# Recurrent mixer of a bidirectional encoder: the work of a block is timed from its own x projection, with four gate buffers, fixed padded convolution inputs and the convolution ranked first

## The chip, the cores and the metric

The kernel runs on one core of one Trainium2 chip. The metric is the device time of one execution in microseconds (us). Three runs of the kernel before took 2115.84, 2116.88 and 2120.38 us; their median is 2116.88 us.

## The reference

An encoder trunk of two residual layers on 256 tokens of width 2048, all in float32. Layer 0 mixes tokens by grouped-query attention, layer 1 by a recurrent block; a SwiGLU network of width 5632 follows each. The change concerns the recurrent mixer alone:

```python
xy = h @ w_in                                   # 2048 -> 2 x 2048
xb, yb = jnp.split(xy, 2, axis=-1)
yb = jax.nn.gelu(yb, approximate=True)
xb = depthwise_conv_centred(xb, conv_w, conv_b) # width 4, over time
h_fwd = rg_lru(xb, w_a[0], b_a[0], w_i[0], b_i[0], lam[0], reverse=False)
h_bwd = rg_lru(xb, w_a[1], b_a[1], w_i[1], b_i[1], lam[1], reverse=True)
out = (h_fwd + h_bwd).astype(h.dtype) * yb
return out @ w_out

# rg_lru: r, i = sigmoid(block_diag(x, w_a) + b_a), sigmoid(block_diag(x, w_i) + b_i)
# a = exp(-8 r softplus(-lam)); u = sqrt(1 - a^2) * (i * x); h_t = a_t h_{t-1} + u_t
```

The gate projections are block diagonal: 8 blocks of 256 channels, each with its own four 256 x 256 matrices (two directions, r and i).

## The kernel before, in words

Activations lie with features on the 128 partitions and the 256 tokens along the free axis. A float32 product is made of three float32r products: each operand is split into hi (rounded) and lo (the rest), and hi x hi, hi x lo and lo x hi are summed in PSUM. Weights arrive by DMA in halves of 8 tiles (`raw`, 512 KB, L92); ACT casts a half to `hi` (L93), VectorE subtracts to get `lo` (L94); each has 5 buffers.

**PE** is the only engine whose order is written out by hand; all others are ordered at build time by a scheduler that estimates times, and by priority, which follows the order of the code. What an engine then gets is a fixed queue: it executes in that order, and an instruction that waits holds up everything behind it.

A **step** is one of the 16 pieces of contraction of a projection. In the mixer `project_sum` issues three matmuls of 128x256 per step (L166 to L168). After each step a clock counts up, and at most one piece of work that is due is issued there; `later(t, fn)` makes `fn` due t steps on.

The mixer works in **blocks** of 256 channels (two tiles of 128). An iteration b (L633) first projects the x branch of block b+1 (`conv_branch`, two projections, 32 steps), then the gate branch of block b (`gelu_branch`, two projections, 32 steps). Between these steps stands the work of block b, by the list `WHEN`: four gates (`gates`, 12 matmuls each, L166 to L168 on `pm<-xs`), four `decay`, four `scan`, then `gelu` and two `finish`. In detail:

- `conv_branch` (L530): VectorE scales the projection into the middle of a padded tile `cb` (L535), whose borders POOL sets to zero (L533, L534). ACT makes the first of four taps `xc` (L537), VectorE adds the other three (L539) and splits the sum into `xs` (L203, L204), which the gates' matmuls read.
- `gates` (L583): matmuls on `xs`, then on ACT a Sigmoid per tile into `sg` (and a Tanh into `th` for the r gates); for the i gates POOL multiplies by `xc` (L599).
- `load_gates` (L556): a DMA into `graw` (256 KB, 2 buffers), ACT's cast `ghi` (L564), POOL's `glo` (L565). With 3 buffers the weights of gate n+3 are loaded once gate n's matmuls have been issued.
- `decay` (L606): Exp on ACT, a square (L610), VectorE's product `th` (L611).
- `scan` (L613): Sqrt on ACT, VectorE's `th` times gate (L616), the scan itself (L619 forward, L621 backward), POOL's sum of the two directions (L622).
- `gelu` (L575) and `finish` (L625): Sigmoid of the gate branch, products on POOL (for the last block on VectorE), split into `act` tiles for the output projection, which starts with 44 steps that need no tile of the last block.

Sigmoid and Tanh, Exp, and Sqrt belong to different activation tables, and `table_op` chains all table users in the order of the code, so that on ACT a block's four Exp come after the Sigmoid of its last gate.

Of the kernel before, what the change touches and what calls it, by code (L numbers as in the profile page):

```python
# [15 lines left out]
ALU = mybir.AluOpType  # L16
AX = mybir.AxisListType

P = 128
S = 256  # L20
# [19 lines left out]
VALUE = 32  # L40
USUAL = (17, 22, 15, 7)
LATE = ((10, 23, 15, 13), (4, 15, 17, 9))
GATE_BUFS = 3
WHEN = (18, 25, 32, 39, 42, 46, 50, 54, 58, 60, 62, 64, 66, 70, 74)
WHEN_LAST = (5, 9, 13, 17, 19, 20, 21, 24, 24, 25, 26, 27, 33, 39, 39)
GELU_B = 0.044715

PK = {}
# [11 lines left out]
def trunk(ctx, tc, w, out):  # L60
    nc = tc.nc
    act, dve, pool, pe, sync = nc.scalar, nc.vector, nc.gpsimd, nc.tensor, nc.sync
# [11 lines left out]
    def nm(s):  # L74
        uid[0] += 1
        return f"{s}_{uid[0]}"

    def tmp(tag, shape=(P, S), dt=F32, bufs=2):
        pl = tp if tag in COMMON else scope[-1]
        return pl.tile(list(shape), dt, tag=tag, name=nm(tag), bufs=bufs)  # L80
# [56 lines left out]
    def later(delay, fn):  # L137
        waiting.append((clock[0] + delay, fn))
# [26 lines left out]
    def three(o, hi, lo, x, start, stop):  # L165
        pe.matmul(o, hi, x[:, :S], start=start, stop=False)  # L166
        pe.matmul(o, hi, x[:, S:], start=False, stop=False)  # L167
        pe.matmul(o, lo, x[:, :S], start=False, stop=stop)  # L168

    def project_sum(xs):  # L170
        acc = new_acc()[:, :S]
        for k0 in range(0, len(xs), HALF):
            for k, (hi, lo) in enumerate(half(), k0):
                three(acc, hi, lo, xs[k], k == 0, k == len(xs) - 1)
                step()
        return acc
# [25 lines left out]
    def split(dst, src):  # L202
        dve.tensor_copy(dst[:, :S], src)  # L203
        dve.tensor_tensor(dst[:, S:], src, dst[:, :S].bitcast(F32), ALU.subtract)  # L204
# [17 lines left out]
    def col(name, i):  # L222
        o = PK[name] + i
        return pk[:, o : o + 1]
# [63 lines left out]
    def table_op(i):  # L288
        if prev[0] is not None:
            tc.add_manual_dep(  # L290
                i.ins, prev[0].ins.name,
                mybir.DependencyInfo(mybir.DependencyClass.NoSync, mybir.DependencyReason.DATA),
                reason="activation tables",
            )
        prev[0] = i

    def table_act(*a, **k):
        table_op(act.activation(*a, **k))  # L298
# [228 lines left out]

    rt = ctx.enter_context(ExitStack())
    scope.append(rt.enter_context(tc.tile_pool(name="rp", bufs=2)))
    def conv_branch(ct):  # L530
        acc = project_sum(nr.xs)
        b = tmp("cb", (P, S + 4))
        pool.memset(b[:, 0:2], 0.0)  # L533
        pool.memset(b[:, S + 2 : S + 4], 0.0)  # L534
        dve.tensor_tensor(b[:, 2 : S + 2], acc, nr.r, ALU.mult)  # L535
        xc = tmp("xc", bufs=4)
        act.activation(xc, b[:, 0:S], AF.Identity, bias=col("conv_b", ct), scale=col("conv_w", ct))  # L537
        for k in range(1, 4):
            dve.scalar_tensor_tensor(xc, b[:, k : k + S], col("conv_w", KT * k + ct), xc, ALU.mult, ALU.add)  # L539
        xs = tmp("xs", (P, 2 * S), F32R, bufs=4)  # L540
        split(xs, xc)
        return xc, xs

    def gelu_branch(ct):
        acc = project_sum(nr.xs)
        y = tmp("fg")
        dve.tensor_tensor(y, acc, nr.r, ALU.mult)
        t = tmp("fu")
        act.activation(t, y, AF.Square)
        dve.scalar_tensor_tensor(t, t, 1.0 / GELU_B, y, ALU.add, ALU.mult)  # L550
        return y, t
# [4 lines left out]
    def load_gates(n):  # L556
        if n >= 4 * NBLK:
            return
        b, g = divmod(n, 4)
        lo = tmp("glo", (P, 4, P), F32R, bufs=GATE_BUFS)  # L560
        hi = tmp("ghi", (P, 4, P), F32R, bufs=GATE_BUFS)
        raw = tmp("graw", (P, 4, P), bufs=2)
        sync.dma_start(out=raw, in_=w["w_gates"][b, :, 4 * g : 4 * g + 4, :])
        act.copy(hi, raw)  # L564
        pool.tensor_tensor(lo, raw, hi[:].bitcast(F32), ALU.subtract)  # L565
        gate_w[n] = hi, lo

    class Block:
# [6 lines left out]
        def gelu(self):  # L575
            table_op(act.preload_act_table_set("sigmoid_and_others"))
            for y, t in self.ys:
                table_act(t, t, AF.Sigmoid, scale=2.0 * GELU_C * GELU_B)
                gl = tmp("gl")
                self.eng.tensor_tensor(gl, y, t, ALU.mult)  # L580
                self.gls.append(gl)

        def gates(self, g):  # L583
            b = self.b
# [2 lines left out]
            for j in range(2):  # L587
                o = pst[:, j * S : (j + 1) * S]
                for k in range(2):
                    m = 2 * k + j  # L590
                    x = self.xcs[k][1]
                    three(o, hi[:, m, :], lo[:, m, :], x, k == 0, k == 1)
            load_gates(4 * b + g + GATE_BUFS)
            for j in range(2):
# [18 lines left out]
        def scan(self, d, j):  # L613
            a, th = self.gate[d, j], self.th[d, j]
            table_act(th, th, AF.Sqrt)
            dve.tensor_tensor(th, th, self.gate[2 + d, j], ALU.mult)  # L616
            h = tmp("h", bufs=4)
            if d == 0:
                dve.tensor_tensor_scan(h, a, th, 0.0, ALU.mult, ALU.add)  # L619
            else:  # L620
                dve.tensor_tensor_scan(h[:, ::-1], a[:, ::-1], th[:, ::-1], 0.0, ALU.mult, ALU.add)  # L621
                self.eng.tensor_tensor(self.hs[j], self.hs[j], h, ALU.add)  # L622
            self.hs.setdefault(j, h)
# [7 lines left out]
    units = [(d, j) for j in range(2) for d in range(2)]  # L631
    blk = nxt = None
    for b in range(-1, NBLK):  # L633
        blk, nxt = nxt, Block(b + 1) if b + 1 < NBLK else None
        if blk:
            work = [partial(blk.gates, g) for g in range(4)]
            work += [partial(blk.decay, *u) for u in units]
            work += [partial(blk.scan, *u) for u in units]
            work += [blk.gelu] + [partial(blk.finish, j) for j in range(2)]
            when = WHEN if nxt else WHEN_LAST  # L640
            for t, fn in zip(when, work):
                later(t, fn)
        if nxt:
            nxt.xcs = [conv_branch(2 * b + 2 + i) for i in range(2)]
            if not blk:
                for g in range(GATE_BUFS):
                    load_gates(g)
        if blk:
            blk.ys = [gelu_branch(2 * b + i) for i in range(2)]

    def end_recurrence():
        rt.close()
        scope.pop()
# [71 lines left out]
```

## Time and profile before

| | |
|---|---|
| median of three runs | 2116.88 us |
| the profiled execution | 2129.33 us, of which 2127.6 us are the span of the profile |
| PE busy | 2085.5 us (98%) |
| VectorE (DVE) busy | 1502.9 us (71%) |
| ACT busy | 1050.4 us (49%) |
| POOL busy | 473.4 us (22%) |
| mixer, from the first gate matmul to the first matmul of the output projection | 1063.31 to 1293.72 us |

The profiled execution is 12.4 us longer than the median; durations are taken from it, and differences are carried over to the median. A row of a timeline has start, duration, engine, line and operation, output <- inputs, and in brackets the idle time before it with what ended it. A duration overlaps the next start a little, so the time that an operation costs in a full queue is read from start to start. A row of waits has the total, the count and the longest.

### The profile page before, as it was taken

How to read it: one execution, taken by the hardware profiler on the slowest of the kernel's cores; microseconds unless marked ns; L12 is line 12 of the kernel's file. 1: busy time of each engine (PE TensorE's matmuls, PEld its weight loads, DVE VectorE, ACT ScalarE, POOL GpSimd, SP SyncE). 2: the span in 40 equal slices, each digit the busy share in tenths (PEclk: the TensorE clock that was granted, in tenths of full speed). 3: DMA queues.
4: the chain of work that ended last, by engine and by line, in shares of the span. 5: the costliest groups of instructions: out<-in, count | busy, mean ns of one | idle time of the engine just before them, and what ended most of it. 6: DMA issues, size and time to landing. Idle time of an engine off the chain costs nothing.

```text
span 2127.6 us, 32676 instructions
## 1 busy us (share of the span) xinstructions
PE 2085.5 (98%) x12512; PEld 1848.4 (87%) x12512; DVE 1502.9 (71%) x2192; ACT 1050.4 (49%) x1598; POOL 473.4 (22%) x454
## 2 busy tenths in 40 slices
PE   7899999999999999999999998999999999999999
PEld 6788888888888888888999997888888888888888
DVE  8899876666566666668889898866666566666665
ACT  5465544443344434444587877454443444444442
POOL 5564431110011100113345553411110011001100
PEclk9999999999999999999999999999999999999999
DMA  6433655555555555555645454555555555665564
GB/s 239 146 122 118 203 187 189 185 185 186 187 188 188 173 186 195 188 183 177 196 160 169 161 166 157 185 188 190 190 194 189 189 189 187 183 203 190 188 189 138
DMA packets 112045, 384.27 MB, mean 181 GB/s; under 512 B 12560, under 2 KB 14736, under 8 KB 111888
## 3 DMA queue, kind: packets, MB, share of 16 engines
q1 hardware_dynamic: 111744, 382.17, 54.4%
q8 instruction: 98, 1.61, 0.3%
q14 instruction: 59, 0.48, 0.1%
q10 hardware_dynamic: 144, 0.02, 0.0%
HBM read 380.04 MB, written 2.10 MB: 180 GB/s over the span
## 4 chain that ended last, share of the span: by engine, by line
PE 86%; DVE 6%; issue 3%; ACT 2%; DMA 1%; POOL 1%; SPq 0%; ACTq 0%; DVEq 0%; POOLq 0%
PE acc L155 53%; PE acc L156 27%; DVE lo L94 2%; DMA graw<-in_w_gates_dram 1%; PE acc L168 1%; PE acc L167 1%; ACT sg L298 1%; PE acc L166 1%; PE pm L167 1%; POOL hb L351 1%; DVE xc L539 1%; PE pm L168 1%; DVE h L621 1%; ACT hi L93 1%; PE pm L166 1%
## 5 line engine op out<-in xcount | busy, mean ns | idle before, releaser
L94 DVE TENSOR_TENSOR lo<-raw,hi 128x1024 fp32r<-128x1024 f32 (+2 forms) x721 | 901.0, 1250 | 509.0 <-ACT hi L93 495.8
L93 ACT CAST hi<-raw 128x1024 fp32r<-128x1024 f32 (+2 forms) x721 | 740.8, 1029 | 928.2 <-PE acc L155 533.6
L155 PE MATMUL acc<-xg,hi 128*128 128x512 f32 x3200 | 1133.1, 398 | 5.7 <-ACT hi L93 5.7
L156 PE MATMUL acc<-xg,lo 128*128 128x256 f32 x3200 | 900.7, 281 | 5.4 <-DVE lo L94 5.4
L155 PEld LDWEIGHTS acc<-xg,hi 128*128 128x128 f32 x3200 | 603.4, 189 | 144.3 <-ACT hi L93 5.7
L155 PE MATMUL acc<-act,hi 128*128 128x512 f32 x1892 | 664.9, 396 | 4.6 <-DVE act L204 4.6
L156 PEld LDWEIGHTS acc<-xg,lo 128*128 128x128 f32 x3200 | 607.8, 190 | 7.1 <-DVE lo L94 7.0
L156 PE MATMUL acc<-act,lo 128*128 128x256 f32 x1892 | 530.9, 281 | 0.4 <-DVE lo L94 0.4
L155 PEld LDWEIGHTS acc<-act,hi 128*128 128x128 f32 x1892 | 355.8, 188 | 87.8 <-DVE act L204 5.5
L497 POOL TENSOR_TENSOR fg<-fg,nr 128x256 f32<-128x256 f32 x88 | 126.1, 1433 | 1189.9 <-ACT fg L298 1189.9
L156 PEld LDWEIGHTS acc<-act,lo 128*128 128x128 f32 x1892 | 358.4, 189 | 0.7 <-DVE lo L94 0.7
L168 PE MATMUL acc<-xg,lo 128*128 128x256 f32 x512 | 146.0, 285 | 3.0 <-DVE lo L94 3.0
L166 PE MATMUL acc<-xg,hi 128*128 128x256 f32 x512 | 146.4, 286 | 2.2 <-ACT hi L93 2.2
L167 PE MATMUL acc<-xg,hi 128*128 128x256 f32 x512 | 145.9, 285 | 0.0
L168 PEld LDWEIGHTS acc<-xg,lo 128*128 128x128 f32 x512 | 99.2, 194 | 3.8 <-DVE lo L94 3.8
L166 PEld LDWEIGHTS acc<-xg,hi 128*128 128x128 f32 x512 | 99.2, 194 | 3.1 <-ACT hi L93 3.1
L167 PEld LDWEIGHTS acc<-xg,hi 128*128 128x128 f32 x512 | 99.1, 194 | 0.0
L280 DVE TENSOR_TENSOR x<-x,acc 128x256 f32<-128x256 f32 x126 | 52.9, 420 | 57.8 <-PE acc L156 57.8
L254 POOL TENSOR_TENSOR ss<-ss,sq 128x256 f32<-128x256 f32 x60 | 78.1, 1302 | 4.9 <-ACT sq L250 0.7
L252 POOL TENSOR_TENSOR sq<-x 128x256 f32<-128x256 f32 x45 | 34.6, 769 | 114.6 <-DVE x L281 112.6
L244 DVE SCALAR_TENSOR_TENSOR xg<-x,pk,xg 128x256 fp32r<-128x256 f32 x64 | 56.2, 891 | 5.2 <-POOL xg L243 5.2
L351 POOL TENSOR_TENSOR hb<-hy,rope 32x256 f32<-32x256 f32 x60 | 46.1, 769 | 44.7 <-DVE hv L419 37.9
(164 smaller groups left out, 1486.6 us busy)
## 6 DMA issues: line engine op xcount, KB each, us to landing
raw<-in_w_gate_dram SPq DMA_DIRECT2D x176, 512.0 KB, 3.6
raw<-in_w_up_dram SPq DMA_DIRECT2D x176, 512.0 KB, 3.6
raw<-in_w_down_dram SPq DMA_DIRECT2D x128, 512.0 KB, 3.6
raw<-in_w_in_dram SPq DMA_DIRECT2D x64, 512.0 KB, 4.0
raw<-in_w_down_dram SPq DMA_DIRECT2D x64, 384.0 KB, 3.1
raw<-in_w_qv_dram SPq DMA_DIRECT2D x40, 512.0 KB, 3.7
raw<-in_w_o_dram SPq DMA_DIRECT2D x32, 512.0 KB, 3.6
raw<-in_w_out_dram SPq DMA_DIRECT2D x32, 512.0 KB, 3.7
```

Source lines behind the costliest of these rows:

```text
L93: act.copy(hi[:, sl, :], raw[:, sl, :])
L94: dve.tensor_tensor(lo[:, sl, :], raw[:, sl, :], hi[:, sl, :].bitcast(F32), ALU.subtract)
L155: pe.matmul(acc, hi, xs[k], start=(k == 0), stop=False)
L156: pe.matmul(acc[:, S:], lo, xs[k][:, :S], start=False, stop=(k == total - 1))
L166: pe.matmul(o, hi, x[:, :S], start=start, stop=False)
L167: pe.matmul(o, hi, x[:, S:], start=False, stop=False)
L168: pe.matmul(o, lo, x[:, :S], start=False, stop=stop)
L244: dve.scalar_tensor_tensor(t[:, S:], x_sb[k], g, t[:, :S].bitcast(F32), ALU.mult, ALU.subtract)
L254: pool.tensor_tensor(self.ss, self.ss, sq, ALU.add)
L280: dve.tensor_tensor(x_sb[j], x_sb[j], acc[:, :S], ALU.add)
L351: eng.tensor_tensor(b[32 * j : 32 * j + 32], y[32 * i : 32 * i + 32], s[32 * i : 32 * i + 32], ALU.mult)
L497: pool.tensor_tensor(g, g, norm.r, ALU.mult)
```

## The change

- `GATE_BUFS` goes from 3 to 4: the weights of gate n+4 are loaded once gate n's matmuls are issued, a whole block ahead.
- The work of a block is no longer started at the head of the iteration after its x branch, but right after its own x branch. The times in `WHEN` count from there: gates at 20, 27, 34, 41 (for the first block 12 less), `decay` and `scan` behind them. `gelu` and `finish` have a list of their own, `WHEN_OUT`, that counts from the end of the gate branch.
- The padded tiles are two fixed ones, cleared once; POOL's 32 small memsets go.
- The convolution behind its projection gets a priority raised by 200.
- Two products are written in place (the GELU product into `y`, the backward scan into its gate tile), so the buffers of `gl` and half of `h` go.

```diff
-GATE_BUFS = 3
-WHEN = (18, 25, 32, 39, 42, 46, 50, 54, 58, 60, 62, 64, 66, 70, 74)
-WHEN_LAST = (5, 9, 13, 17, 19, 20, 21, 24, 24, 25, 26, 27, 33, 39, 39)
+GATE_BUFS = 4
+WHEN = (20, 27, 34, 41, 44, 47, 50, 53, 57, 59, 61, 63)
+FIRST_BLOCK = 12
+AHEAD = 200
+WHEN_OUT = (2, 6, 10)
...
+    padded = [tmp(f"cb{i}", (P, S + 4), bufs=1) for i in range(2)]
+    for b in padded:
+        pool.memset(b, 0.0)
+
     def conv_branch(ct):
         acc = project_sum(nr.xs)
-        b = tmp("cb", (P, S + 4))
-        pool.memset(b[:, 0:2], 0.0)
-        pool.memset(b[:, S + 2 : S + 4], 0.0)
+        with tc.high_priority(offset=AHEAD):
+            return conv(ct, acc)
+
+    def conv(ct, acc):
+        b = padded[ct % 2]
         dve.tensor_tensor(b[:, 2 : S + 2], acc, nr.r, ALU.mult)
...
-                gl = tmp("gl")
-                self.eng.tensor_tensor(gl, y, t, ALU.mult)
-                self.gls.append(gl)
+                self.eng.tensor_tensor(y, y, t, ALU.mult)
+                self.gls.append(y)
...
-            h = tmp("h", bufs=4)
+            h = tmp("h") if d == 0 else self.gate[2 + d, j]
...
-        if blk:
-            work = [partial(blk.gates, g) for g in range(4)]
-            work += [partial(blk.decay, *u) for u in units]
-            work += [partial(blk.scan, *u) for u in units]
-            work += [blk.gelu] + [partial(blk.finish, j) for j in range(2)]
-            when = WHEN if nxt else WHEN_LAST
-            for t, fn in zip(when, work):
-                later(t, fn)
         if nxt:
             nxt.xcs = [conv_branch(2 * b + 2 + i) for i in range(2)]
             if not blk:
                 for g in range(GATE_BUFS):
                     load_gates(g)
+            work = [partial(nxt.gates, g) for g in range(4)]
+            work += [partial(nxt.decay, *u) for u in units]
+            work += [partial(nxt.scan, *u) for u in units]
+            for t, fn in zip(WHEN, work):
+                later(t if blk else t - FIRST_BLOCK, fn)
         if blk:
             blk.ys = [gelu_branch(2 * b + i) for i in range(2)]
+            for t, fn in zip(WHEN_OUT, [blk.gelu] + [partial(blk.finish, j) for j in range(2)]):
+                later(t, fn)
```

What this makes of the queues, at three places of a middle block. In the rows a name's numbers tell its buffer and its place in the code. First PE's queue at the first gate of a block, before; `xs_1890` and `xs_1922` are the convolution outputs that this gate reads, and `acc_1967` is the second x projection of the next block:

```order
L166 MATMUL acc_1967_10909<-xg_1704_9507,hi_1969_10911 128x256
L167 MATMUL acc_1967_10909<-xg_1704_9507,hi_1969_10911 128x256
L168 MATMUL acc_1967_10909<-xg_1704_9507,lo_1970_10912 128x256
L166 MATMUL pm_1971_10922<-xs_1890_10477,ghi_1908_10561 128x256
L167 MATMUL pm_1971_10922<-xs_1890_10477,ghi_1908_10561 128x256
L168 MATMUL pm_1971_10922<-xs_1890_10477,glo_1907_10560 128x256
L166 MATMUL pm_1971_10922<-xs_1922_10629,ghi_1908_10561 128x256
```

The same gate now; `acc_2015` is the second gate-branch projection, 20 steps after the block's own x projections:

```order
L168 MATMUL acc_2015_11172<-xg_1722_9605,hi_2017_11174 128x256
L169 MATMUL acc_2015_11172<-xg_1722_9605,hi_2017_11174 128x256
L170 MATMUL acc_2015_11172<-xg_1722_9605,lo_2018_11175 128x256
L168 MATMUL pm_2019_11191<-xs_1992_11009,ghi_1951_10786 128x256
L169 MATMUL pm_2019_11191<-xs_1992_11009,ghi_1951_10786 128x256
L170 MATMUL pm_2019_11191<-xs_1992_11009,glo_1950_10785 128x256
L168 MATMUL pm_2019_11191<-xs_2005_11103,ghi_1951_10786 128x256
```

The gate has moved from 50 steps to 20 steps behind the end of its x projections, and its matmuls 4 and on read the second convolution's output.

Second, VectorE's queue from the second `cb` of a block to that convolution's `xs`, before:

```order
L535 TENSOR_TENSOR cb_2072_11478<-acc_2043_11338,nr_1857_10276 128x256
L94 TENSOR_TENSOR lo_2110_11684<-raw_2108_11682,hi_2109_11683 128x1024
L539 SCALAR_TENSOR_TENSOR xc_2073_11482<-cb_2072_11478,pk_79,xc_2073_11482 128x256 x3
L203 CAST xs_2074_11487<-xc_2073_11482 128x256
L204 TENSOR_TENSOR xs_2074_11487<-xc_2073_11482,xs_2074_11487 128x256
```

Now, in two pieces; `th_1954`, `th_1965`, `th_1956` and `th_1967` and the scans belong to the block before, `cb0` and `cb1`, `xc_1991` and `xc_2004` to the new block. The first piece starts at the first product that needs a Sqrt:

```order
L624 TENSOR_TENSOR th_1954_10793<-th_1954_10793,sg2_1978_10905 128x256
L548 SCALAR_TENSOR_TENSOR xc_1991_11004<-cb0_1832_10215,pk_79,xc_1991_11004 128x256
L96 TENSOR_TENSOR lo_2029_11232<-raw_2027_11230,hi_2028_11231 128x1024
L544 TENSOR_TENSOR cb1_1833_10216<-acc_1993_11012,nr_1859_10280 128x256
L624 TENSOR_TENSOR th_1965_10847<-th_1965_10847,sg3_1987_10965 128x256
L627 SCALAR_TENSOR_TENSOR h_2002_11062<-sg0_1953_10791,th_1954_10793 128x256
L624 TENSOR_TENSOR th_1956_10797<-th_1956_10797,sg2_1979_10908 128x256
L548 SCALAR_TENSOR_TENSOR xc_1991_11004<-cb0_1832_10215,pk_79,xc_1991_11004 128x256
L624 TENSOR_TENSOR th_1967_10851<-th_1967_10851,sg3_1988_10968 128x256
L96 TENSOR_TENSOR lo_2043_11295<-raw_2041_11293,hi_2042_11294 128x1024
L629 SCALAR_TENSOR_TENSOR sg3_1987_10965<-sg1_1964_10845,th_1965_10847 128x256
L548 SCALAR_TENSOR_TENSOR xc_2004_11098<-cb1_1833_10216,pk_79,xc_2004_11098 128x256
```

The second piece follows at once and ends with the second `xs`:

```order
L627 SCALAR_TENSOR_TENSOR h_2003_11082<-sg0_1955_10795,th_1956_10797 128x256
L205 CAST xs_1992_11009<-xc_1991_11004 128x256
L96 TENSOR_TENSOR lo_2052_11358<-raw_2050_11356,hi_2051_11357 128x1024
L629 SCALAR_TENSOR_TENSOR sg3_1988_10968<-sg1_1966_10849,th_1967_10851 128x256
L556 TENSOR_TENSOR fg_2013_11167<-acc_2006_11106,nr_1859_10280 128x256
L548 SCALAR_TENSOR_TENSOR xc_2004_11098<-cb1_1833_10216,pk_79,xc_2004_11098 128x256
L206 TENSOR_TENSOR xs_1992_11009<-xc_1991_11004,xs_1992_11009 128x256
L96 TENSOR_TENSOR lo_2066_11434<-raw_2064_11432,hi_2065_11433 128x1024
L548 SCALAR_TENSOR_TENSOR xc_2004_11098<-cb1_1833_10216,pk_79,xc_2004_11098 128x256
L559 SCALAR_TENSOR_TENSOR fu_2014_11169<-fu_2014_11169,fg_2013_11167 128x256
L205 CAST xs_2005_11103<-xc_2004_11098 128x256
L206 TENSOR_TENSOR xs_2005_11103<-xc_2004_11098,xs_2005_11103 128x256
```

Where one convolution stood as a piece behind the scans of the block before, both are now threaded between that block's products, its four scans and four `lo`.

Third, ACT's queue now, from the weights' cast that waits for the last gate of the block (`pm_1983`) to its first Sqrt:

```order
L573 CAST ghi_1985_10960<-graw_1986_10961 128x512
L300 ACTIVATE sg3_1987_10965<-pm_1983_10946,pk_79 128x256
L300 ACTIVATE sg3_1988_10968<-pm_1983_10946,pk_79 128x256
L300 ACT_TABLE_LOAD
L300 ACTIVATE sg0_1953_10791<-sg0_1953_10791,ncs_2435 128x256
...
L618 ACTIVATE sq_1989_10984<-sg0_1953_10791 128x256
L95 CAST hi_2017_11174<-raw_2016_11173 128x1024
L618 ACTIVATE sq_1990_10997<-sg1_1964_10845 128x256
L546 ACTIVATE xc_1991_11004<-cb0_1832_10215,pk_79 128x256
...
L300 ACT_TABLE_LOAD
L300 ACTIVATE th_1954_10793<-th_1954_10793 128x256
```

Left out are three more Exp and two more squares. Between the last gate and the first Sqrt stand the two Sigmoid, a table load, four Exp, four squares, one `hi`, one `xc` and a second table load. Before, the same stretch has three `hi` and a GELU square where this has one `hi` and one `xc`.

## The prediction

> **What bounds the kernel now.** I read the page first, then the busy time by stretch, the waits of TensorE (PE), and last the timelines of ACT and VectorE (DVE). The page's part 1 gives PE 98% of the span. Where the rest goes, the busy time by stretch shows: the first row is the recurrent mixer (1050 to 1315 us), the second one undisturbed block of it:
>
> ```profile
> 1050.00:1315.00 265.00, 249.17 (x1975) 243.65 (x1974) 230.95 (x333) 208.09 (x365) 122.53 (x131) 0.98 0.49 161
> ...
> 1104.54:1136.91 32.37, 32.37 (x273) 32.37 (x273) 28.04 (x41) 25.36 (x45) 16.82 (x18) 1.00 0.50 164
> ...
> sum 159.96, PE 151.50 PEld 149.25 DVE 142.96 ACT 126.79 POOL 84.34; mean PE 30.30 PEld 29.85 DVE 28.59 ACT 25.36 POOL 16.87
> ```
>
> The columns after the length are PE, PEld, DVE, ACT and POOL, then granted clock, DMA share and GB/s. In the mixer PE idles 265.0 - 249.2 = 15.8 us and loses 0.02 x 265 = 5.3 us to a lowered clock: 21 us, all that a better order could win here. 32.37 us / 273 = 0.119 us is the spacing of one 256-column matmul, so the 240 matmuls of a steady block (64 steps of three, four gates of twelve) need 28.6 us. The sum row spans five cycles of the waiting chain, 32.0 us each. VectorE is busy for 28.6 of these: beside PE there is no second engine with room to spare. Who ends PE's waits from 1050 to 1330 us:
>
> ```profile
> PE pm L168 <- POOL glo L565: 4.2, 4, 1.1
> PE acc L155 <- DVE act L204: 3.7, 1, 3.7
> PE acc L168 <- DVE lo L94: 3.0, 4, 0.8
> PE pm L166 <- ACT ghi L564: 2.3, 1, 2.3
> PE acc L166 <- ACT hi L93: 2.2, 3, 1.6
> ```
>
> Gate weights (glo, ghi) end 6.5 us, the split weights (hi, lo) 5.2 us, the last gated tiles (act) 3.7 us. None waits for xs, the split output of the convolution. A wait also costs afterwards:
>
> ```profile
> 1164.02:1168.00 3.98, 3.98 (x33) 3.98 (x34) 3.95 (x7) 3.41 (x7) 1.43 (x3) 1.00 0.45 153
> ...
> 1283.09:1289.57 6.48, 5.44 (x24) 5.15 (x25) 6.45 (x6) 3.51 (x8) 6.40 (x6) 0.50 0.27 86
> 1313.74:1320.00 6.26, 6.26 (x27) 5.41 (x28) 4.41 (x8) 3.33 (x5) 1.87 (x2) 0.74 0.50 179
> ```
>
> After a wait of 1.1 us (first row) the clock stays at 1.00. After 3.70 us it is 0.74 over 6.26 us, that is half rate for 3.3 us, 1.65 us lost. The row at 1283 starts after a wait of 2.3 us and holds another of 1.0: half rate for all of 6.5 us.
>
> **The change, part by part.** Fourth gate buffer: the loads of a gate's weights start a whole block ahead, so the 6.5 us for glo and ghi go. Fixed padded buffers: 32 small POOL memsets go, and with them POOL's waits at them; nothing is added. Products written in place: the same operations on other tiles, nothing. GELU moved to its own place: one activation-table load more per block, 1.28 us on ACT, which otherwise waits for the next gate at that point; its cover is that wait, and without it I count 0.3 us below.
>
> What costs is the move of the gates. They stood 18 steps into the next block, 50 steps after the convolution's input was complete; now the first comes 20 steps after it, 20 x 3 x 0.119 = 7.1 us. VectorE's new order (shown with the change) has 24 operations from the first decay product th (L624) of block b to the end of block b+1's second xs (L206). That th needs the Sqrt of block b; Sqrt needs Exp, and Exp follows the Sigmoid of b's last gate in ACT's order. So there is a ring: last gate of b, ACT chain, VectorE chain, xs, first gate of b+1, three more gates, last gate of b+1. I price its three arcs.
>
> ACT arc. Its rows now, with the same operations in one cycle:
>
> ```profile
> 1233.29 0.60 ACT L537 ACTIVATE xc<-cb,pk 128x256 f32<-128x256 f32 x1 [1.42 <-DVE cb L535]
> ...
> 1236.71 0.62 ACT L564 CAST ghi<-graw 128x512 fp32r<-128x512 f32 x1 [1.58 <-DMA graw<-in_w_gates_dram]
> 1237.23 0.83 ACT L298 ACTIVATE sg<-pm,pk 128x256 f32<-128x256 f32 x2
> 1238.08 1.28 ACT L298 ACT_TABLE_LOAD   x1
> 1239.38 1.71 ACT L298 ACTIVATE sg<-sg,ncs 128x256 f32<-128x256 f32 x4
> 1240.99 1.03 ACT L93 CAST hi<-raw 128x1024 fp32r<-128x1024 f32 x1
> 1241.93 1.02 ACT L610 ACTIVATE sq<-sg 128x256 f32<-128x256 f32 x3
> ...
> 1244.11 0.40 ACT L549 ACTIVATE fu<-fg 128x256 f32<-128x256 f32 x1
> 1244.42 1.03 ACT L93 CAST hi<-raw 128x1024 fp32r<-128x1024 f32 x1
> 1245.47 1.28 ACT L298 ACT_TABLE_LOAD   x1
> 1246.76 1.34 ACT L298 ACTIVATE th<-th 128x256 f32<-128x256 f32 x4
> ```
>
> From ghi (1236.71) to VectorE's th (1247.29, below) is 10.58 us. The new arc has two hi fewer (0.94 each, 1240.99 to 1241.93), one square fewer (0.31) and one xc more (0.60): 9.0 us. ACT reaches ghi some 0.3 us after the gate, since a table load and a hi now stand before it, and POOL's late products hold VectorE a little: 9.4.
>
> VectorE arc:
>
> ```profile
> 1058.58 0.42 DVE L535 TENSOR_TENSOR cb<-acc,nr 128x256 f32<-128x256 f32 x1
> 1058.91 1.22 DVE L94 TENSOR_TENSOR lo<-raw,hi 128x1024 fp32r<-128x1024 f32 x1
> 1060.05 1.52 DVE L539 SCALAR_TENSOR_TENSOR xc<-cb,pk,xc 128x256 f32<-128x256 f32 x3
> ...
> 1062.62 0.29 DVE L203 CAST xs<-xc 128x256 fp32r<-128x256 f32 x1
> 1062.94 0.43 DVE L204 TENSOR_TENSOR xs<-xc,xs 128x256 fp32r<-128x256 f32 x1
> ```
>
> ```profile
> 1228.74 0.47 DVE L539 SCALAR_TENSOR_TENSOR xc<-cb,pk,xc 128x256 f32<-128x256 f32 x1
> 1229.14 0.41 DVE L204 TENSOR_TENSOR act<-h,act 128x256 fp32r<-128x256 f32 x1
> ...
> 1247.29 0.76 DVE L616 TENSOR_TENSOR th<-th,sg 128x256 f32<-128x256 f32 x2
> 1247.96 0.42 DVE L547 TENSOR_TENSOR fg<-acc,nr 128x256 f32<-128x256 f32 x1
> 1248.30 0.75 DVE L616 TENSOR_TENSOR th<-th,sg 128x256 f32<-128x256 f32 x2
> 1248.97 0.68 DVE L619 TENSOR_TENSOR_SCAN h<-sg,th 128x256 f32<-128x256 f32 x1
> 1249.57 0.67 DVE L621 TENSOR_TENSOR_SCAN h<-sg,th 128x256 f32<-128x256 f32 x1
> 1250.15 1.17 DVE L619 TENSOR_TENSOR_SCAN h<-sg,th 128x256 f32<-128x256 f32 x1
> 1251.24 1.16 DVE L621 TENSOR_TENSOR_SCAN h<-sg,th 128x256 f32<-128x256 f32 x1
> ```
>
> By start-to-start times: four th at 0.34, four lo at 1.14, four scans at 0.60, five xc at 0.40, cb, fg and fu at 0.33, two xs at 0.6: 1.4 + 4.6 + 2.4 + 2.0 + 1.0 + 1.2 = 12.5 us (rounded). The last two scans took 1.09 instead of 0.60, while POOL was at work; two POOL sums fall into the arc, so 13.5.
>
> PE arc, from xs to the end of the fourth gate: the first gate's other 9 matmuls, three times 21 of projection, three gates of 12: 108 x 0.119 = 12.9 us, plus 1.65 at half rate: 14.5.
>
> The ring takes 9.4 + 13.5 + 14.5 = 37.4, say 37 us per block, where now 32.0 pass and PE needs 28.6. PE waits at the fourth matmul of the first gate; the rest of the GELU projection and the other gates stand behind it in PE's queue, and ACT and POOL wait for those.
>
> **The sum**, from points of the trace:
>
> ```profile
> 1063.31 0.28 PE L166 MATMUL pm<-xs,ghi 128*128 128x256 f32 x1
> ...
> 1293.72 0.40 PE L155 MATMUL acc<-act,hi 128*128 128x512 f32 x1
> ...
> 1313.74 0.80 PE L155 MATMUL acc<-act,hi 128*128 128x512 f32 x1 [3.70 <-DVE act L204]
> ```
>
> Block 0's xs is complete at 1063.4 (1062.94 + 0.43), just when its gate wants it (1063.31). VectorE's order up to there is unchanged, but the gate now stands ten steps earlier, so PE waits 3.3 us for the same moment. Then 14.5 to the last gate of block 0 (1077.9); ACT 9.9 (one hi more than later) and a shorter VectorE arc of 6.8 (one lo only) to block 1's xs: 1094.6. Six rings of 37 us: 1316.6. Rest of block 6: 57 matmuls and a half-rate stretch, 8.4; block 7: 120 matmuls, 14.3. The output projection starts at 1339.3 instead of 1293.72: 45.6 us later. There the last block's tiles are wanted 23 + 44 steps of 0.357 us after its last gate, 23.9 us, and its two arcs take 9.4 + 13.5 = 22.9, so the wait of 3.7 us, the 0.4 us before it and the 1.65 us behind it should mostly go: I give back 5. Net +40.6 us on an execution of 2129.33 us (span 2127.6). The runs' median is 2116.88, 12.4 lower; I carry the difference over: 2157 us.
>
> The Trainium skill, "ScalarE: Activation LUTs", section "What ACT_TABLE_LOAD costs", gives 2.66 us for a switch of table set, half of it a drain. The rows above contradict it here: Exp starts 1.30 us after its load (1238.08, 1239.38). By the page the ring, with two loads, would be 2.7 us longer and the sum some 19 us higher.
>
> Bounds. Below: no contention, no half rate, no 0.4 us: 9.0 + 12.5 + 12.9 = 34.4 us; started at 1092.4, six of them and the rest (6.8 + 14.3) end at 1319.9, 26 us late, less 5.7: +20, 2137. Above: 40 us, with half rate for 6.5 us as at 1283 and two more POOL collisions: started at 1096, it ends at 1360, +62 after the 5 are given back, 2179. A measurement of this kernel tells about 0.2%, 4 us, from no change.
>
> **The rivals.** Faster: xs is ready in time. Then the buffers and memsets win what they are meant to, all 15.8 + 5.3 us and the 1 us of slow clock after 1315: 2095. It decides at 15.7 us (43 steps of 0.357 and three matmuls), the time between the last gate of b and the fourth matmul of the next first gate; the arcs need 21.5 at their shortest. For it speaks that the convolution carries a rank of 200: were VectorE's operations freely ordered, xs would need only some 4 us after its projection. Against it, the order is fixed, with all scans ahead. 5%.
>
> No change: the new wait only replaces the old ones. The ring would have to be 32 us, 2.4 below its shortest sum. 2%.
>
> Short ring: VectorE meets POOL nowhere and the clock stays up, 34.4 us, 2137. The clock row at 1313 speaks against it. 15%.
>
> Long ring, 39 us and more, 2170 or beyond: half rate outlasts the first gate, because PE waits twice, once for each xs. The row at 1283 speaks for it. 15%.
>
> **How the numbers follow.** My forecast, ring of 35.5 to 39 us, has 63%, and 2157 us. Range 2135 to 2179: it leaves out the faster and the equal case and the outer end of the long ring, some 15%. Slower 0.93, faster 0.05, same 0.02.
>
> **What would show it.** PE's waits must name DVE xs (L206) first, with 6 to 8 us per block and some 50 in all, and glo and ghi must be gone. The spacing of blocks should be about 37 us, the clock below 1 after each first gate, VectorE's share lower in the mixer, the wait at act near nothing. If PE shows no wait for xs, or waits of under 3 us, the ring is wrong.

## The result, and the profile after

The changed kernel takes 2171.20 us (median of four runs, 2165.07 to 2175.44), the kernel before 2117.71 (median of four, 2115.84 to 2120.38): a ratio of 1.0249, 95% interval 1.0220 to 1.0279. The profiled executions lie 44.1 us apart: 2173.42 us (span 2171.6) against 2129.33 (span 2127.6). The busy times of the page, and the waits of TensorE (PE) over the whole span as far as they stand in the mixer (total, count, longest):

```profile
PE 2101.2 (97%) x12512; PEld 1856.0 (85%) x12512; DVE 1474.7 (68%) x2192; ACT 1060.2 (49%) x1605; POOL 456.8 (21%) x424
```

```profile
PE pm L168 <- DVE xs L205: 25.0, 14, 5.5
PE pm L169 <- DVE xs L206: 19.0, 7, 2.8
```

The waits for glo, ghi, hi and lo are gone from the mixer, and 44 us of waits for xs stand there instead. VectorE's share fell from 71% to 68%, although PE now waits for VectorE. One block of the changed kernel as a stretch (length, then PE, PEld, DVE, ACT, POOL busy, granted clock, DMA share, GB/s), and PE's waits in it:

```profile
1163.64:1201.18 37.54, 31.93 (x241) 31.06 (x241) 24.76 (x41) 26.86 (x46) 14.25 (x14) 0.91 0.42 141
```

```profile
1163.64 0.39 PE L168 MATMUL pm<-xs,ghi 128*128 128x256 f32 x1 [1.51 <-DVE xs L205]
1166.86 0.58 PE L169 MATMUL pm<-xs,ghi 128*128 128x256 f32 x1 [2.83 <-DVE xs L206]
1168.92 0.58 PE L168 MATMUL pm<-xs,ghi 128*128 128x256 f32 x1 [1.27 <-DVE xs L205]
...
1170.62 0.41 PE L168 MATMUL pm<-xs,ghi 128*128 128x256 f32 x1
1170.84 0.41 PE L169 MATMUL pm<-xs,ghi 128*128 128x256 f32 x1
...
1183.94 0.28 PE L170 MATMUL pm<-xs,glo 128*128 128x256 f32 x1
...
1342.49 0.40 PE L157 MATMUL acc<-act,hi 128*128 128x512 f32 x1
```

The period of 37.5 us is constant to 0.02 us. Each block has three waits, 5.6 us in all: for the first xs (cast), for its rest (split), and for the second xs. After them matmuls stand 0.21 us apart instead of 0.119. 1183.94 is the last matmul of the fourth gate, 1342.49 the start of the output projection. ACT from the cast ghi that waits for the third gate on (the one at 1184.45 stands behind the fourth):

```profile
1180.21 0.62 ACT L573 CAST ghi<-graw 128x512 fp32r<-128x512 f32 x1 [0.37 <-PE pm L169]
...
1184.45 0.61 ACT L573 CAST ghi<-graw 128x512 fp32r<-128x512 f32 x1
1184.97 0.83 ACT L300 ACTIVATE sg<-pm,pk 128x256 f32<-128x256 f32 x2
...
1187.11 1.71 ACT L300 ACTIVATE sg<-sg,ncs 128x256 f32<-128x256 f32 x4
...
1192.81 0.42 ACT L300 ACTIVATE th<-th 128x256 f32<-128x256 f32 x1
```

and VectorE (DVE), from the second xs of one block to that of the next:

```profile
1168.90 0.43 DVE L206 TENSOR_TENSOR xs<-xc,xs 128x256 fp32r<-128x256 f32 x1
...
1186.71 0.81 DVE L205 CAST act<-h 128x256 fp32r<-128x256 f32 x1 [0.63 <-POOL h L635]
...
1193.38 0.41 DVE L624 TENSOR_TENSOR th<-th,sg 128x256 f32<-128x256 f32 x1
...
1206.45 0.43 DVE L206 TENSOR_TENSOR xs<-xc,xs 128x256 fp32r<-128x256 f32 x1
```

The ring is read off these rows. From the end of the second xs (1168.90 + 0.43 = 1169.33) to the end of the fourth gate (1183.94 + 0.28 = 1184.22) 14.9 us on PE; from there to the first th 9.2 us on ACT (1193.38 - 1184.22); from th to the end of the next second xs (1206.88) 13.5 us on VectorE. The sum is 37.55, the period. It has to be, as the three stretches join end to end; that they are a ring, the joints show. PE waits for the second xs. ACT last idles at the ghi behind the third gate (1180.21), works without a pause from there to Sqrt, and comes to the ghi behind the fourth gate 0.2 us after that gate's end. The first th starts 0.15 us after the end of Sqrt (1192.81 + 0.42), and VectorE has no idle from there to xs.

The granted clock has a part in the period, too:

```profile
1163.30:1166.71 3.41, 0.39 (x1) 0.19 (x1) 3.41 (x6) 0.42 (x1) 0.85 (x2) 1.00 0.43 148
1166.71:1173.54 6.83, 5.41 (x22) 4.95 (x23) 2.59 (x6) 2.22 (x3) 1.27 (x1) 0.50 0.35 115
1173.54:1204.26 30.72, 26.52 (x220) 26.12 (x218) 22.18 (x35) 24.64 (x44) 12.98 (x13) 1.00 0.43 146
1204.26:1211.08 6.82, 5.41 (x22) 4.94 (x23) 2.58 (x6) 2.22 (x3) 1.27 (x1) 0.50 0.32 118
```

In this profile the clock changes only on a grid of 3.41 us. The step up to 1166.71 holds a single matmul; then PE has half rate for two steps and the full rate for nine. Eleven steps are 37.55 us. Of PE's 14.9 us the half rate costs some 2, an estimate: at 0.119 us apart the 107 matmuls from the second xs to the end of the fourth gate take 12.7.

For the experiments I use one row, the group of all casts of xs, with the first and last start. Before, from 1057.9 to 1268.6, 210.7 us; changed, from 1057.6 to 1318.8, 261.2 us:

```profile
L203 DVE CAST xs<-xc x16: 286/306/787, 1057.9 to 1268.6; 128x256 fp32r<-128x256 f32 x16
```

```profile
L205 DVE CAST xs<-xc x16: 265/286/1422, 1057.6 to 1318.8; 128x256 fp32r<-128x256 f32 x16
```

Below, "length" is this distance, and "spacing" the mean distance between the casts of the second xs of blocks 2 to 7 in VectorE's timeline (five periods): 31.99 us before, 37.54 changed.

### The profile page after: what moved, and what is told of

Its sections match the earlier page's. It is cut to its first block, busy times and chain, and to the rows that moved or that the text cites. A ratio compares the mean times of both kernels' runs of the same rounds, so it can differ in the third digit from the quotient of the medians.

```text
span 2171.6 us, 32687 instructions
## 1 busy us (share of the span) xinstructions
PE 2101.2 (97%) x12512; PEld 1856.0 (85%) x12512; DVE 1474.7 (68%) x2192; ACT 1060.2 (49%) x1605; POOL 456.8 (21%) x424
## 4 chain that ended last, share of the span: by engine, by line
PE 43%; DVE 4%; POOL 1%; issue 1%; ACT 1%; DVEq 0%; POOLq 0%
PE acc L157 25%; PE acc L158 12%; PE acc L168 1%; PE acc L169 1%; PE acc L170 1%; DVE lo L96 1%; PE pm L168 1%; DVE xc L548 1%; PE pm L169 1%; PE pm L170 1%; DVE sg L629 0%; POOL h L635 0%; DVE act L206 0%; ACT th L300 0%; DVE h L627 0%
## 5 line engine op out<-in xcount | busy, mean ns | idle before, releaser
L168 PE MATMUL acc<-xg,hi 128*128 128x256 f32 x512 | 149.2, 291 | 0.0
L169 PE MATMUL acc<-xg,hi 128*128 128x256 f32 x512 | 148.6, 290 | 0.0
L574 POOL TENSOR_TENSOR glo<-graw,ghi 128x512 fp32r<-128x512 f32 x32 | 45.9, 1434 | 93.2 <-ACT ghi L573 90.5
L168 PE MATMUL pm<-xs,ghi 128*128 128x256 f32 x128 | 40.8, 319 | 25.0 <-DVE xs L205 25.0
```

## The experiments

My theory was the ring: last gate, ACT to Sqrt, VectorE from th over the scans to xs, first gate of the next block. Rivals: VectorE is simply too full beside PE; the first gate stands too soon after its own projection (20 steps); the other parts of the change cost. The first two runs add the same work to VectorE at two places.

**Work added inside the ring** (pad_in). In `scan`:

```diff
             dve.tensor_tensor(th, th, self.gate[2 + d, j], ALU.mult)
+            for _ in range(2):
+                dve.tensor_tensor(th, th, th, ALU.max)
```

> The changed kernel with eight more VectorE operations in each block (th is taken as the maximum of itself and itself, which leaves its value), two between each product th and its scan, so inside the arc from Sqrt to xs. By the start-to-start time of th, 0.34 us, they are 2.7 us. Ring theory: blocks come 2.7 us further apart, 40.2 us instead of 37.54, and the mixer is some 19 us longer (seven arcs). Rival, VectorE merely too full: the same as in the run with the operations outside the ring.

```profile
1201.63 0.93 DVE L206 TENSOR_TENSOR xs<-xc,xs 128x256 fp32r<-128x256 f32 x1
1227.13 0.41 DVE L624 TENSOR_TENSOR th<-th,sg 128x256 f32<-128x256 f32 x1
...
1242.43 0.93 DVE L206 TENSOR_TENSOR xs<-xc,xs 128x256 fp32r<-128x256 f32 x1
```

```profile
1197.70:1207.94 10.24, 6.70 (x28) 6.12 (x29) 4.83 (x10) 3.33 (x6) 3.68 (x3) 0.50 0.19 64
```

Length 278.0 us (1045.9 to 1323.9), 16.8 more; spacing 40.76, 3.2 more (second xs to second xs in these rows, 40.8). VectorE's arc took 16.2 us (1227.13 to 1243.36), 2.7 more, as worked out; the other 0.5 us is in PE's arc, where the half rate now lasts three steps instead of two.

**The same work outside it** (pad_out), behind the second xs:

```diff
         split(xs, xc)
+        for _ in range(8 if ct % 2 else 0):
+            dve.tensor_tensor(xc, xc, xc, ALU.max)
```

> The changed kernel with the same eight operations more in each block, now on xc right behind the second xs, outside the ring: VectorE idles 6.8 us there for the next hi. Ring theory: blocks stay at 37.5 us (within 0.3), the mixer within 3 us of the changed kernel's. Rival, VectorE too full: 2.7 us a block here too.

```profile
1194.10 4.63 DVE L552 TENSOR_TENSOR xc<-xc 128x256 f32<-128x256 f32 x8
1200.84 1.23 DVE L96 TENSOR_TENSOR lo<-raw,hi 128x1024 fp32r<-128x1024 f32 x1 [2.11 <-ACT hi L95]
```

Here the eight took even 4.63 us, and behind them VectorE still idles 2.1 us: length 261.5 (1044.7 to 1306.2), spacing 37.73, 0.2 more, and no more than the 37.75 of the second profile of this kernel without added work (norank, below). VectorE isn't too full; what counts is where on it an operation stands. Single profiled executions took 2181.36 and 2172.16 us.

**One piece taken out of the ring** (lateact). An order-only dependency (`behind`) puts the split of act behind the newest xs; the two forward scans follow it there:

```diff
 WHEN_OUT = (2, 6, 10)
+OUT_MID = (2, 33, 34)
...
+            i = dve.tensor_copy(g[:, :S], h)
+            if self.b < NBLK - 2:
+                behind(i, last_xs[0])
```

> The changed kernel with one thing turned round in VectorE's order: the split of the gated tiles (act) of blocks 0 to 5 stands behind the second xs of the block after next, and the two forward scans, which wait for its tile, go there with it; th, Sqrt and the backward scans stay ahead of xs. Of the arc from the first th to xs that takes out two scans, 1.2 us. Ring theory (last gate, Sqrt, th, xs): blocks come 1.2 us closer, every 36.0 to 36.6 us. Rival ring (third gate, GELU, POOL's product, act, and VectorE's unbroken 20 us behind it): act is 2.9 us and the scans 1.2 us of it, so blocks come every 33 to 34 us if the first ring is not nearly as long. Rival, VectorE too full: 37.5 us.

```profile
1164.56 0.42 DVE L561 TENSOR_TENSOR xs<-xc,xs 128x256 fp32r<-128x256 f32 x1
...
1188.83 0.42 DVE L635 TENSOR_TENSOR th<-th,sg 128x256 f32<-128x256 f32 x1 [0.59 <-ACT th L301]
...
1199.86 0.42 DVE L561 TENSOR_TENSOR xs<-xc,xs 128x256 fp32r<-128x256 f32 x1
```

Length 248.5 (1056.9 to 1305.4), spacing 35.48: 2.1 us less, between the two forecasts. In this kernel the rows decide for the first ring: th now waits 0.59 us for Sqrt on an idle VectorE, and VectorE's arc is 11.45 us (1188.83 to 1200.28), 2.05 shorter. I had counted the two scans alone (1.2 us); POOL's two sums left the arc with them, and the cast of xs and one tap xc, which had taken 0.68 and 0.83 us beside a sum, took 0.20 and 0.39. In the changed kernel the act split with VectorE's unbroken work behind it (from 1186.71) reached th at the same moment as Sqrt: the two ways were tied. 2173.03 us against 2141.29 of the kernel before in the same session, ratio 1.0161 (1.0110 to 1.0211). That the first gate stands too soon falls as the sole cause: its distance is the same, the spacing isn't.

**The ring's PE arc shortened** (tight), the gates moved together:

```diff
-WHEN = (20, 27, 34, 41, 44, 47, 50, 53, 57, 59, 61, 63)
+WHEN = (20, 23, 26, 29, 44, 47, 50, 53, 57, 59, 61, 63)
```

> The changed kernel with the four gates of a block at 20, 23, 26 and 29 steps instead of 20, 27, 34 and 41: the first gate stands where it stood, and PE has 12 steps (36 matmuls, 4.3 us) more between the last gate of a block and the first of the next. Ring theory: PE's arc of the ring falls by 36 x 0.119 = 4.3 us and VectorE's by up to 1.9 (three operations now stand ahead of the first th), ACT may queue up by 1; blocks come every 32 to 33.5 us instead of 37.5, and the time falls by 24 to 34 us, to about 2140 to 2148. Rival, the first gate too soon after its own projection: nothing changes, since that distance is the same, and the time stays within 5 us of 2171. Rival, VectorE too full: no change either, its work is the same.

```profile
1203.42 0.83 ACT L300 ACTIVATE sg<-pm,pk 128x256 f32<-128x256 f32 x2
1204.27 1.28 ACT L585 ACT_TABLE_LOAD   x1
...
1209.58 0.42 ACT L300 ACTIVATE fu<-fu 128x256 f32<-128x256 f32 x1 [1.40 <-DVE fu L559]
1210.02 1.28 ACT L300 ACT_TABLE_LOAD   x1
1211.32 1.71 ACT L300 ACTIVATE sg<-sg,ncs 128x256 f32<-128x256 f32 x4
```

A miss: length 259.6 (1045.4 to 1305.0), spacing 37.71; 2167.06 us, ratio 1.0214 (1.0177 to 1.0250). The PE arc did fall, to 10.2 us, and VectorE's to 11.5, but the ACT arc rose from 9.2 to 16.0: GELU's sigmoids, which had stood ahead of the last gate, now stand between it and Exp, and wait for VectorE's fu. Exp starts 7.9 us after the last gate's Sigmoid instead of 2.1.

**GELU taken out of that place** (tightg):

```diff
-WHEN = (20, 27, 34, 41, 44, 47, 50, 53, 57, 59, 61, 63)
+WHEN = (20, 23, 26, 29, 44, 47, 50, 53, 57, 59, 61, 63)
...
-WHEN_OUT = (2, 6, 10)
+WHEN_OUT = (33, 37, 41)
+OUT_LAST = (2, 6, 10)
```

> The gates at 20, 23, 26 and 29 again, and GELU's two sigmoids moved behind the block's Sqrt (33 steps after the projection instead of 2; in the last block as it was). With the tight gates alone blocks still came every 37.7 us, since GELU, whose projection ends at step 32, then stood between the last gate and Exp in ACT's order. Ring theory: with GELU out of that place the ring is shorter by the 36 matmuls (4.3 us) and by a table load and two sigmoids (2.0 us), and by what VectorE no longer has ahead of xs; blocks come every 30 to 33 us, the waits for xs fall below 3 us a block, and the time is 2122 to 2145. Rival, the first gate too soon behind its own projection, or VectorE too full: blocks stay at 36 us or more, 2160 to 2175.

```profile
1195.61 0.43 DVE L207 TENSOR_TENSOR xs<-xc,xs 128x256 fp32r<-128x256 f32 x1
1215.66 0.42 DVE L625 TENSOR_TENSOR th<-th,sg 128x256 f32<-128x256 f32 x1
...
1233.28 0.43 DVE L207 TENSOR_TENSOR xs<-xc,xs 128x256 fp32r<-128x256 f32 x1
```

Missed again: length 260.9 (1047.2 to 1308.1), spacing 37.71; 2173.93 us, ratio 1.0211 (1.0145 to 1.0276). PE 10.1 and ACT 9.5 us are as foreseen, but the later GELU brought the act split and more lo into VectorE's arc: 18.05 us (1215.66 to 1233.71). My forecast had not counted the new order. That tight lies so near the changed kernel is chance as far as the rows show: its five distances all lie between 37.70 and 37.72. Those of tightg fall from 37.93 to 37.57; norank, below, shows towards what.

**All but the new gate times** (lategates):

```diff
-WHEN = (20, 27, 34, 41, 44, 47, 50, 53, 57, 59, 61, 63)
-FIRST_BLOCK = 12
+WHEN = (50, 57, 64, 71, 74, 78, 82, 86, 90, 92, 94, 96)
+WHEN_LAST = (37, 41, 45, 49, 51, 52, 53, 56, 56, 57, 58, 59)
+FIRST_BLOCK = 32
```

> All of the change but the new gate times: gates, decay and scans at the steps at which they stood before (50 steps after the convolution's input; in block 0 and the last block as before), with four gate buffers, fixed padded buffers, products in place and GELU at its own place. VectorE's order in the mixer is that of the kernel before. Ring theory: PE waits for no xs, glo and ghi no longer end a wait, blocks come every 30 to 32 us, and the time is that of the kernel before less 3 to 12 us: 2105 to 2115. Rival, the other parts cost (one table load more a block, 1.28 us of ACT in eight blocks, or in-place products): slower than before by 5 us or more.

```profile
PE acc L171 <- DVE lo L97: 3.8, 5, 0.8
...
PE acc L169 <- ACT hi L96: 3.4, 3, 1.5
PE acc L158 <- DVE fg L557: 2.8, 1, 2.8
```

2116.99 us, ratio 1.0002 (0.9980 to 1.0024): no wait for xs, glo or ghi, length 209.2 (1046.0 to 1255.2), 1.5 less than before. So the whole loss is the move of the gates, and the buffers and memsets win next to nothing: the 6.5 us for glo and ghi went, but lo, hi and a new wait for fg took most of it back, and PE's waits sum to 14.8 us instead of 15.8.

**xs ahead of the scans** (xsfirst), th products and scans of blocks 1 to 6 put behind the next second xs (the steps of the scans in `WHEN` move to 66, 68, 70 and 72 for it, here and in free):

```diff
+            if 0 < self.b < NBLK - 1:
+                tc.add_manual_dep(
+                    i.ins, last_xs[0].ins.name,
...
```

> The changed kernel, with VectorE's order alone turned round in blocks 1 to 6: the last Sqrt products th and the four scans of a block stand behind the next block's second xs instead of ahead of it (an order-only dependency; the same operations). Ring theory: the arc from Sqrt over the scans to xs is cut out, what is left of the ring is ACT's way to its second xc (9.4 us and about 2 more) and some 5.3 us of VectorE, 16.7 against the 15.7 us that stand between a block's last gate and the next need of xs; so the waits for xs fall from 5.6 to about 1 us a block, blocks come every 29 to 31 us instead of 37.5, and the time falls by 40 to 60 us, to 2110 to 2130. Rival, VectorE too full beside PE (no order helps): the wait stays at 4 us a block or more, and the time falls by less than 12 us. Rival, the gates simply stand too soon after the projection (20 steps, 7.1 us): the wait stays too, since cb, xc and xs still follow the projection.

```profile
PE pm L169 <- DVE xs L553: 20.9, 8, 5.5
PE pm L170 <- DVE xs L554: 3.7, 7, 2.0
```

Spacing 32.22, length 229.9 (1057.8 to 1287.7): 31.3 us of the 50.5 are won back; 2141.42 us, ratio 1.0100 (1.0074 to 1.0126). The direction is right, the size is not: 24.6 us of waits for xs remain, where I expected about 1 a block. VectorE now works from act to xs, 15.8 us (1176.46 to 1192.25), with one pause of 0.33 us, which led to two more runs:

```profile
1176.46 0.82 DVE L206 CAST act<-h 128x256 fp32r<-128x256 f32 x1 [0.64 <-POOL h L645]
...
1191.83 0.42 DVE L554 TENSOR_TENSOR xs<-xc,xs 128x256 fp32r<-128x256 f32 x1
```

**Sqrt moved behind xc on ACT** (free), and **act behind xs too** (free2):

```diff
+            if mid:
+                behind(i, last_xc[0])
```

> The run xsfirst, and in ScalarE's order too the four Sqrt of blocks 1 to 6 stand behind the next block's second xc. In xsfirst blocks came every 32.3 us on average, and VectorE worked without a break from the split of the gated tiles (act, at 1176.46 us) to xs: the ring seems to run there over GELU, POOL's product and act, not over Sqrt. Ring theory: moving Sqrt off ACT's way alone changes little, blocks come every 31 to 32.5 us. Rival, ACT's Sqrt ahead of xc is what was left: blocks come every 29 to 30 us.

> The run free, and the split of the gated tiles (act) of blocks 0 to 5 too is put behind the second xs of the block after next. Now nothing of an earlier block stands ahead of xs on VectorE but the four th of the decay. Ring theory: no ring is left that is longer than PE's own 28.6 us; PE waits for no xs in blocks 1 to 6 or for less than 0.7 us a block, blocks come every 28.8 to 30.3 us, and the time is 2098 to 2118, at or below the kernel before. Rival, ACT (26.8 us busy a block) or VectorE (25.7) too full: blocks stay at 31 us or more, 2125 to 2142.

```profile
1197.47 0.62 ACT L585 CAST ghi<-graw 128x512 fp32r<-128x512 f32 x1 [3.17 <-PE pm L171]
1200.08 1.04 ACT L97 CAST hi<-raw 128x1024 fp32r<-128x1024 f32 x1 [1.99 <-PE acc L171]
...
1202.44 0.47 ACT L302 ACTIVATE sg<-pm,pk 128x256 f32<-128x256 f32 x1
```

Both slower than xsfirst: spacing 33.40 and 34.71, lengths 235.6 (1058.5 to 1294.1) and 242.1 (1056.8 to 1298.9); 2160.66 us in the one execution of free, 2164.53 and a ratio of 1.0098 (1.0066 to 1.0129) for free2. For free both forecasts were too low, that of the rival by far. For free2 the theory that no ring would be left fell; its rival's 31 us or more came true, the time that went with it (2125 to 2142) did not. The rows (of free2) show a next one: a cast hi that waits for PE to release a weight buffer now stands ahead of the first gate's Sigmoid, which starts 5.0 us after its ghi.

**Sqrt put back, act left behind xs** (xsact):

> VectorE's order of the run free2 (th products, scans and act behind the second xs), with ScalarE's Sqrt left ahead of xc as in xsfirst. In free2 blocks came every 34.8 us: ACT stood 2.0 us at a cast hi that waits for a weight buffer and that now stands ahead of the first gate's sigmoids, and worked without a break from there to xc. That order of hi and sigmoid is the same in this kernel. If this queue on ACT is what was left, blocks come every 33.5 to 35.5 us here too, and the time is some 1% above the kernel before. If free2 lost its time by the moved Sqrt instead, blocks come every 30 to 32.3 us, as in xsfirst or better.

Spacing 33.62, length 237.8 (1059.0 to 1296.8), 2160.05 us, ratio 1.0109 (1.0059 to 1.0159): within the forecast for ACT's queue. That this hi is the cause is argued from the queue and these two kernels; no run moved it alone.

**The rank** (norank): `AHEAD = 0`, with which every engine's instructions stand in the same order.

> The changed kernel with the convolution's rank set to 0. Every engine's instructions stand in the same order as with 200, so this is also a second, longer measurement of the changed kernel: blocks at 37.5 us and no difference in the mixer (within 1 us). What its runs decide is how the changed kernel spreads: if the stages outside the mixer go at the two paces that the profiles show (a pair of matmuls every 0.347 or 0.353 us), the runs should lie between 2160 and 2178 with some near 2161; if the lower pace comes with the change, all lie above 2168.

Spacing 37.75, length 263.0 (1047.4 to 1310.4), 2171.45 us (median of six, 2163.55 to 2176.36), ratio 1.0191 (1.0137 to 1.0246). The rank does nothing here. All runs lie in the first forecast's 2160 to 2178, though none quite near 2161; the second, all above 2168, falls.

Read as distances, this profile shows more. Its five are 38.04, 37.80, 37.68, 37.61 and 37.60 us, those of pad_out and tightg fall in the same way, and those of pad_in rise from 40.47 to 40.93: towards 11 and 12 steps of the clock, 37.55 and 40.96. Arcs of fixed length would keep one distance. A reading that fits: the clock comes back on its grid, not when xs comes, and each us at half rate costs PE 0.44 us (0.214 us per matmul against 0.119). A block whose xs comes late finds less half rate left, and about half of its delay is made up in the next (0.49, 0.25, 0.13 and 0.06 above 37.55). So in these kernels the clock seems to hold the period to a whole number of its steps, and rings of somewhat different length are drawn to the same one. No run moved the clock by itself, and the distances of tight and lateact do not settle on a whole number.

**The kernel before once more** (before_again):

> The kernel before, unchanged, for a second profiled execution. The first one took 2129.33 us, 12.4 above the median of its runs. If that was chance of this one execution, the profile now shows about 2117 us and the stage that is shorter by some 12 us names where the first lost them. If the profiled execution is always slower than the others, it shows 2127 to 2131 again. In both cases the recurrent mixer should show the waits of the first profile (glo, ghi, hi, lo, act; none for xs).

Neither: 2140.02 us. Length 210.7 (1057.4 to 1268.1) and the mixer's waits as in the first profile, so the time went outside the mixer. Two stretches there, one ahead of the mixer and one behind it, in the first profile of before:

```profile
600.00:700.00 100.00, 100.00 (x568) 86.73 (x567) 63.65 (x90) 44.46 (x62) 13.14 (x9) 1.00 0.56 187
...
1600.00:1700.00 100.00, 100.00 (x579) 88.15 (x578) 60.11 (x76) 40.04 (x44) 2.92 (x2) 1.00 0.56 190
```

in this second one:

```profile
600.00:700.00 100.00, 100.00 (x568) 86.69 (x567) 63.37 (x90) 44.21 (x61) 13.16 (x9) 1.00 0.55 186
...
1600.00:1700.00 100.00, 100.00 (x568) 86.77 (x567) 58.94 (x74) 38.48 (x41) 2.92 (x2) 1.00 0.56 187
```

and the first of them in lategates:

```profile
600.00:700.00 100.00, 100.00 (x579) 88.19 (x578) 63.47 (x90) 45.68 (x64) 13.16 (x9) 1.00 0.58 190
```

PE is busy throughout and its granted clock reads 1.00, yet it gets through 568 or 579 matmuls in 100 us, 1.9% apart. The kernel before went at the lower pace up to the mixer in its first profile and in both stretches in its second; lategates went at the higher, and its first xs comes at 1046.0 instead of 1057.9. These 11.9 us account for the 12.4 by which the first profile lay above its median, if the other executions went at the higher pace; none of them was profiled. In the mixer the two kernels do not differ in pace: matmuls stand 0.119 us apart in both.

## Why the prediction was right and where it failed

**Sign and place: right.** The ring was there. Forecast 9.4 + 13.5 + 14.5 = 37.4, measured 9.2 + 13.5 + 14.9 = 37.55. It leaves PE at the third gate, by a hair: the fourth has 0.2 us in hand. The forecast had the low clock in it, but with 1.65 us a block where some 2 are lost, and nothing of the clock's grid: if it holds the period, as norank's distances suggest, the sum came out this close partly by luck, since 37.4 lay next to eleven steps. The two runs with added work show that it is a ring on VectorE's order and no lack of VectorE, lateact that shortening it shortens the period, lategates that nothing else in the change costs.

**The points on the way.** Block 1's second xs is complete at 1094.3 (forecast 1094.6). The output projection starts at 1342.49 (forecast 1339.3): most of the 3.2 us are six rings of 37.54, which I had rounded to 37. Behind it 4.8 us are given back (span less that start: 833.9 before, 829.1 now; forecast 5). Net 44.1 on the profiled executions, forecast 40.6.

**What failed: the carry to the median.** I took the 12.4 us by which the profile of before lay above its median off the new kernel too. Its own profile lies 2.2 above its median. That is 10.2 of the 13.7 us by which the forecast was low (2157.5 unrounded, measured 2171.2); the ring's 3.5 are the rest. The profile of the changed kernel was at the lower pace up to the mixer and at the higher behind it, like that of before, so 44.1 compares like with like. Its ten executions (norank's included) all lie at 2163.55 or above, although at the higher pace throughout some 2161 would be due (2173.4 less 11.9, an estimate); why none of them came to it, while the kernel before reached its own in most runs beside them, stays open. In two other sessions the kernel before itself had medians of 2141 and 2142.

**The waits: right in sum, wrong in detail.** I named the split of xs (L206) first, with 6 to 8 us a block and some 50 in all; it was 5.6 us a block and 44 in all, and the cast (L205) led with 25.0: three waits in a row, since VectorE's queue has a lo and a scan between them.

**The rivals.** The short ring left out collisions with POOL and the low clock; both were there (the cast and the tap beside POOL's sums, and some 2 us of half rate). The long ring's condition came true, as the half rate outlasts the first gate by 2.3 us (1171.26 to 1173.54), but its 39 us did not. The faster one rested on winning all 21 us of before; lategates has the new buffers, no wait for xs and none of that gain.

**The clock.** Matmuls stood 0.21 us apart behind waits of 1.51, 2.83 and 1.27 us. The Trainium skill, "TensorE: Matmul & The Clock Gate", "Part 1: The HAM clock gate", has half rate set in after at least one idle window of about 3.4 us. The trace agrees in the length of the window, but it need not be idle throughout: no single wait of a steady block was so long, and the window ahead of the drop at 1166.71 holds a matmul, 0.39 us of busy PE.

**Tables.** By the Trainium skill, "ScalarE: Activation LUTs", "What ACT_TABLE_LOAD costs", two loads would have made the ring 2.7 us longer, an estimate from its 2.66 us a switch. The trace does not bear it out: in the rows of tight Exp starts 1.30 us after its load (1210.02, 1211.32).

## What to carry to other kernels

Where an in-order queue holds a block's late work ahead of the next block's early work, look for a ring through the engines: its period is the sum of its arcs, whatever the busy shares say, and an operation counts only if it stands on it. Cutting one arc rarely gives back the whole: count the arcs anew in the new order of every engine, as another way through the same queues is often nearly as long (here 37.5, 35.5, 32.2 us), and where PE's clock falls in each block it may hold the period to whole steps of its own, as it seems to in tightg. And carry no offset between a profile and a median to another kernel before a second profile has shown where it comes from.

## What the runs showed of the hardware

- In every trace here the granted clock changed only on a grid of 3.41 us. In and around the mixer (1040 to 1350 us, all fourteen traces) it fell to half after each step in which PE was busy for less than 1.58 us and after none with more than 1.66; it came back after each with at least 3.1 us and after none with 3.0 or less.
- Two paces of PE at the same granted clock of 1.00: 568 or 579 matmuls in 100 us of the same code, kept for hundreds of microseconds, worth 11.9 us up to the mixer. What sets them was not found.
- Eight VectorE operations in place, each on the result of the one before, took 4.63 us, 0.58 each (pad_out); th products on separate tiles follow at 0.34.
